# In the second up projection, one weight chunk in four gets its remainder from a DMA that adds instead of a subtraction on the vector engine

## The chip, the cores and the metric

The kernel runs on one core of one Trainium2 chip, in one launch. The core has five engines with instruction queues of their own: PE (matrix products, with weight loads PEld beside them), ACT (activations and copies), DVE (element-wise vector work), POOL and SP (here mostly issuers of DMAs). The queues are in order; engines wait for each other and for DMAs by semaphores. The metric is the time of one execution on the device in microseconds.

## What is computed

Two residual layers over 256 tokens of width 2048, in fp32: a gated mixer and a convolutional FFN, then attention with forget gates and a second FFN, and a final norm. The change touches the up projection of the second FFN, `xn @ w_up` below, with a weight of 2048 x 11264.

```python
def conv_ffn(xn, w_up, conv_w, conv_b, w_down):
    S = xn.shape[1]
    h = xn @ w_up
    hp = jnp.pad(h, ((0, 0), (CONV_W - 1, 0), (0, 0)))
    h = sum(hp[:, k:k + S] * conv_w[k] for k in range(CONV_W)) + conv_b
    gate, val = jnp.split(h, 2, axis=-1)
    return (jax.nn.silu(gate) * val) @ w_down
...
    for l in range(DEPTH):
        ...
        h = h + conv_ffn(rmsnorm(h, f_norm[l]), f_w_up[l], f_conv_w[l], f_conv_b[l], f_w_down[l])
```

## The kernel before

All weights are streamed from DRAM once, in chunks of 128 x 1024 fp32 (512 KB). A product in fp32 accuracy is made from products in the faster format fp32r: each operand is split into a rounded part and a remainder, and the products rounded x rounded, rounded x remainder and remainder x rounded are added up in PSUM. The activations X1 hold both parts side by side (2 x 256 columns). The weights are split as they stream by: for every chunk, ACT writes the rounded part `whi` (L95, a copy from `raw` into a tile of type fp32r), and DVE writes the remainder `wlo` = raw - whi (L96).

`Stream` keeps this in order. Each chunk is an item of a list; at step i it issues the load of item i + 6 on SP (L77), the split of item i + 3 (L95, L96), and the matmuls of item i, and then lets the waiting epilogues go one step further (`advance`). The buffers go round: `raw` has 4 (LOADS - AHEAD + 1), `whi` and `wlo` have 4 each (AHEAD + 1). So the load of a chunk into `raw` has to wait until the chunk four before it has been split, and a split has to wait until PE is through with the chunk four before it.

`feat_block` computes 256 features for all tokens from a block of K / 4 chunks of 128 x 1024: 4 chunks, c = 0 to 3, in the up projection. For a chunk PE runs first 16 products of 128 x 256 with `whi` (two halves of X1 for each of 8 weight tiles), then 8 with `wlo`. Sometimes some of the `whi` products are 512 wide. `ffn_up(l)` runs 44 such blocks for each layer; after blocks 1, 12, 23 and 34 an item without a load stands between (`between`, L676), and in layer 1 one after block 2 that starts `residual_by_token` (L384 to L398), which issues a 1024 KB load of gains on POOL and small DMAs on SP. Each block's epilogue `up_done` scales the sums (L350 to L357), convolves (L659, L663), applies SiLU and gate (L666, L667) and splits the result for the down projection (L283, L284), on ACT and DVE, while the next blocks run.

The order of the work on each engine is the order in which this code is written out; there is no scheduler behind it.

Of the kernel before, what the change touches and what calls it, by code (L numbers as in the profile page):

```python
# [10 lines left out]
F32 = mybir.dt.float32  # L11
F32R = mybir.dt.float32r
I32 = mybir.dt.int32
AF = mybir.ActivationFunctionType
OP = mybir.AluOpType
# [5 lines left out]
KD = D // P  # L21
# [22 lines left out]
class Stream:  # L44


    def __init__(self, nc, pool):
        self.nc, self.pool = nc, pool
        self.items, self.pending = [], []
        self.raw, self.parts = {}, {}  # L50

    def chunk(self, src, mult, at, at_load=None, at_split=None, rows=(1, 1), place=None):


        self.items.append((src, mult, at_load, at_split, at, rows, place))

    def then(self, at_load=None, at_split=None, at_mult=None):
        self.items.append((None, at_mult, at_load, at_split, 0, None, None))
# [21 lines left out]
    def _split(self, i):  # L80
        if self.items[i][3]:
            self.items[i][3]()
        raw = self.raw.pop(i, None)
        if raw is None:
            return
        at, (n, pitch) = self.items[i][4:6]
        hi, lo = (self.pool.tile([P, CHUNK + PAD], F32R, name=k, tag=k)[:, at:at + CHUNK] for k in ("whi", "wlo"))
        raw = raw.rearrange("p (n w) -> p n w", n=n)
        h, l = hi, lo
        if n > 1:  # L90
            h, l = (a[:, :n * pitch].rearrange("p (n w) -> p n w", n=n) for a in (h, l))
        else:
            h, l = h[:, None, :], l[:, None, :]
        h, l = (a[:, :, :raw.shape[2]] for a in (h, l))
        self.nc.scalar.activation(h, raw, AF.Copy)  # L95
        self.nc.vector.tensor_tensor(l, raw, h.bitcast(F32), op=OP.subtract)  # L96
        self.parts[i] = (hi, lo)

    def run(self):
# [46 lines left out]
def build(ctx, tc, d, out):  # L146
# [10 lines left out]
    h = const.tile([P, KD, T], F32, name="h")  # L157
    X1 = const.tile([P, KD, 2 * T], F32R, name="X1")
# [8 lines left out]
    s = Stream(nc, wpool)  # L167
    ph = Phase(tc)

    def main_ps():  # L170
        return psum.tile([P, 2, 512], F32, name="ps", tag="ps", bufs=3)
# [4 lines left out]
    def column(i):  # L176
        return col[:, i:i + 1]


    def mm(o, a, b, start, stop):  # L180
        nc.tensor.matmul(o, a, b, start=start, stop=stop, skip_group_check=True)  # L181
# [6 lines left out]
    def wide_next():  # L188
        return state["wide"].pop(0) if state["wide"] else 0

    def feat_block(src, x, K, done):

        box = {}
        n = K // 4
        for c in range(n):
            def mult(hi, lo, c=c):
                if c == 0:
                    box["ps"], box["both"] = main_ps(), False  # L200
                ps, xx, wide = box["ps"], x(), wide_next()
                box["both"] |= wide > 0

                def rounded(j, m):
                    nonlocal wide
                    w = hi[:, j * 256 + m * P:j * 256 + (m + 1) * P]
                    kt = 4 * c + j
                    if wide > 0:
                        mm(ps[:, m, :], w, xx[:, kt, :], kt == 0, False)
                        wide -= 1  # L210
                    else:
                        for half in range(2):
                            mm(ps[:, m, :T], w, xx[:, kt, half * T:(half + 1) * T], kt == 0 and half == 0, False)

                def remainder(j, m):
                    kt = 4 * c + j
                    mm(ps[:, m, :T], lo[:, j * 256 + m * P:j * 256 + (m + 1) * P], xx[:, kt, :T],
                       False, kt == K - 1)

                for product in (rounded, remainder):  # L220
                    for j in range(4):
                        for m in range(2):
                            product(j, m)
                if c == n - 1:
                    s.start(done(box["ps"], box["both"]))
            s.chunk(src[c], mult, FEAT_AT)

    def tok_block(src, x, done, K=KD):
        tok_blocks([(src, done)], x, K)
# [52 lines left out]
    def two_parts(dst, src):  # L282
        nc.scalar.activation(dst[..., :T], src, AF.Copy)  # L283
        nc.vector.tensor_tensor(dst[..., T:], src, dst[..., :T].bitcast(F32), op=OP.subtract)  # L284
# [65 lines left out]
    def scaled(ps, both, a):  # L350

        src = ps[:, :, :T]
        if both:
            nc.scalar.activation(a, ps[:, :, T:], AF.Copy)
            nc.vector.tensor_tensor(a, ps[:, :, :T], a, op=OP.add)
            src = a
        nc.vector.tensor_tensor(a, src, rB[:, None, :].to_broadcast([P, 2, T]), op=OP.mult)  # L357
# [26 lines left out]
    def residual_by_token():  # L384

        gains = ph.keep("gains", [P, D])
        nc.gpsimd.dma_start(gains, d["final"].to_broadcast([P, D]))
        ways = []
        for tb in range(2):
            for g in range(4):  # L390
                turned = blocks_turned(h[:, 4 * g:4 * g + 4, tb * P:(tb + 1) * P])
                yield
                ways.append(rows_out(f"h{tb}{g}", turned))
                yield
        for tb in range(2):
            for g in range(4):
                yield
                rows_in(by_token()[:, tb, g * 512:(g + 1) * 512].rearrange("p (r x) -> p r x", r=4), ways.pop(0))  # L398
# [243 lines left out]
    def ffn_h():  # L642
        ph.open(f"ffn{state['layer']}")
        return ph.keep("H", [P, KF, 2 * T], F32R)

    def up_done(l, i):
        def done(ps, both):
            state["layer"] = l
            H = ffn_h()
            while state["scaled"] <= l:  # L650
                yield
            a = ph.temp("a", [P, 2, T])
            scaled(ps, both, a)
            yield
            c = ph.temp("c", [P, 2, T])
            for m in range(2):
                f = m * KF + i
                w = [column(C_CONVW + (l * 3 + k) * 2 * KF + f) for k in range(3)]
                nc.scalar.activation(c[:, m, :], a[:, m, :], AF.Identity, scale=w[2],  # L659
                                     bias=column(C_CONVB + l * 2 * KF + f))  # L660
                for k in (1, 0):
                    n = 2 - k
                    nc.vector.scalar_tensor_tensor(c[:, m, n:], a[:, m, :T - n], w[k], c[:, m, n:],  # L663
                                                   op0=OP.mult, op1=OP.add)
            yield
            nc.scalar.activation(c[:, 0, :], c[:, 0, :], AF.Silu)  # L666
            nc.vector.tensor_tensor(c[:, 0, :], c[:, 0, :], c[:, 1, :], op=OP.mult)  # L667
            yield
            two_parts(H[:, i, :], c[:, 0, :])
        return done  # L670

    def ffn_up(l):
        for i in range(KF):
            feat_block(d[f"up{l}"][4 * i:4 * i + 4], lambda: X1, KD, up_done(l, i))
            if i % 11 == 1:
                s.then(at_mult=between)  # L676
            if l and i == 2:
                s.then(at_mult=lambda: s.start(residual_by_token()))
# [279 lines left out]
    for p in range(8):  # L958
        feat_block(d["a_in_u"][4 * p:4 * p + 4], lambda: X1, KD, u_done(p))
    for p in range(8):  # L960
        feat_block(d["a_out"][4 * p:4 * p + 4], mlp_x2, KD, residual(p, C_FNORM, row_scale))
    ffn_up(0)
    for p in range(8):
        feat_block(d["down0"][11 * p:11 * p + 11], ffn_h, KF, residual(p, C_BNORM))
# [13 lines left out]
    for p in range(8):  # L978
        feat_block(d["b_out"][4 * p:4 * p + 4], lambda: att("X2"), KD, residual(p, C_FNORM + KD, row_scale))
    ffn_up(1)  # L980
    s.then(at_mult=between)
    for blk in range(3):
# [72 lines left out]
```

## Time and profile before

| what | value |
|---|---|
| median of 3 runs | 2181.74 us (2180.86 to 2181.95) |
| profiled execution, its time as the profile gives it (span from the first to the last instruction) | 2179.9 us |
| difference of the median from that span | 1.8 us |
| mean granted clock of PE | 0.999 |
| DMA packets | 447.31 MB, mean 205 GB/s |
| loads `raw<-up` (both layers) | 352 of 512 KB, 4.1 us from issue to landing (median) |
| second up projection | from about 1453 us to 1932 us: 44 blocks of 4 chunks |

A row of the timeline gives the start, the duration, the engine, the line of the kernel, the operation and its tiles as out<-in; in brackets stands how long the engine was idle before, and who released it. A row of a group gives count, busy time, mean duration of one and the idle time before them. "To landing" is the time from a DMA's issue until its semaphore says that all of its data is there. The profile's busy times for PE are modelled at their ends, so a burst of matmuls can seem to reach a little into the next.

### The profile page before, as it was taken

What the parts mean: (1) busy time and instruction counts of PE and PEld (TensorE: products, weight loads), DVE (VectorE), ACT (ScalarE), POOL (GpSimd) and SP (SyncE); (2) the same over time, 40 slices, a digit from 0 to 9 for tenths busy, and PEclk for the clock granted to TensorE, in tenths of its full rate; (3) what the DMA queues carried; (4) which work ended last, traced back from release to release, by engine and by line L of the source; (5) the groups of instructions that cost most, each with busy time, mean ns of one, the idle gap of its engine ahead of it and who ended that gap; (6) DMA issues with size and microseconds to landing.
All of it is one profiled execution on the core that took longest, in us unless ns stands there. A gap on an engine that the chain in (4) does not pass through costs nothing.

```text
span 2179.9 us, 45085 instructions
## 1 busy us (share of the span) xinstructions
PE 2170.3 (100%) x18740; PEld 2154.6 (99%) x18740; DVE 1474.8 (68%) x2085; ACT 1145.4 (53%) x1536; POOL 26.9 (1%) x46
## 2 busy tenths in 40 slices
PE   9999999999999999999999999999999999999998
PEld 9999999999999999999999999999999999999998
DVE  6696687777777755556787676678777777764444
ACT  6665555555555544444545665446555555544443
POOL 0000000000000000000001100000000000000000
PEclk9999999999999999999999999999999999999999
DMA  8686566665666666666777776567766666666664
GB/s 311 191 241 202 193 198 195 189 199 190 198 193 194 195 190 199 193 195 184 244 244 257 232 224 200 185 216 228 240 195 194 193 195 189 201 191 194 193 192 153
DMA packets 153229, 447.31 MB, mean 205 GB/s; under 512 B 25584, under 2 KB 44800, under 8 KB 152640
## 3 DMA queue, kind: packets, MB, share of 16 engines
q1 hardware_dynamic: 151488, 440.48, 64.6%
q0 software_dynamic: 1072, 3.41, 0.6%
q8 instruction: 146, 2.39, 0.5%
q10 hardware_dynamic: 464, 0.55, 0.1%
q14 instruction: 59, 0.48, 0.1%
HBM read 430.72 MB, written 13.65 MB: 204 GB/s over the span
## 4 chain that ended last, share of the span: by engine, by line
PE 99%; DMA 0%; DVE 0%; ACT 0%; SPq 0%; issue 0%; DVEq 0%
PE ps L181 98%; PE mp L913 0%; PE ps L907 0%; PE ps L908 0%; PE ps L906 0%; PE mp L912 0%; DMA mlp_vt<-a_in_v 0%; DVE h L491 0%; PE mp L376 0%; ACT whi L95 0%; ACT sq L405 0%; PE mp L181 0%; DVE h L404 0%; SPq L496 0%; DVE h L486 0%
## 5 line engine op out<-in xcount | busy, mean ns | idle before, releaser
L96 DVE TENSOR_TENSOR wlo<-raw,whi 128x1024 fp32r<-128x1024 f32 (+1 forms) x778 | 945.1, 1219 | 462.4 <-ACT whi L95 458.2
L95 ACT ACTIVATE whi<-raw 128x1024 fp32r<-128x1024 f32 (+1 forms) x778 | 819.3, 1058 | 737.8 <-PE ps L181 660.3
L181 PE MATMUL ps<-X,whi 128*128 128x256 f32 (+1 forms) x6476 | 824.0, 279 | 0.0
L181 PEld LDWEIGHTS ps<-X,whi 128*128 128x128 f32 x6476 | 776.2, 188 | 6.5
L181 PE MATMUL ps<-X,wlo 128*128 128x256 f32 x3328 | 445.3, 276 | 0.0
L181 PEld LDWEIGHTS ps<-X,wlo 128*128 128x128 f32 x3328 | 409.9, 188 | 1.6
L181 PE MATMUL ps<-whi,ffn_H 128*128 128x256 f32 (+1 forms) x1402 | 222.7, 277 | 0.0
L181 PEld LDWEIGHTS ps<-whi,ffn_H 128*128 128x128 f32 x1402 | 192.0, 188 | 0.4
L181 PE MATMUL ps<-ffn_H,whi 128*128 128x256 f32 x1408 | 173.9, 276 | 0.0
L663 DVE SCALAR_TENSOR_TENSOR ffn_c<-ffn_a,col,ffn_c 128x255 f32<-128x255 f32 x352 | 161.9, 481 | 6.4
L181 PEld LDWEIGHTS ps<-ffn_H,whi 128*128 128x128 f32 x1408 | 166.1, 188 | 0.0
L181 PE MATMUL ps<-whi,att_X 128*128 128x256 f32 (+2 forms) x970 | 164.3, 285 | 0.0
L181 PE MATMUL ps<-whi,X 128*128 128x256 f32 (+1 forms) x1000 | 157.4, 280 | 0.4 <-ACT whi L95 0.4
L181 PE MATMUL ps<-wlo,ffn_H 128*128 128x256 f32 (+1 forms) x700 | 151.3, 277 | 0.0
L181 PEld LDWEIGHTS ps<-whi,att_X 128*128 128x128 f32 x970 | 135.4, 188 | 3.5
L181 PEld LDWEIGHTS ps<-whi,X 128*128 128x128 f32 x1000 | 133.5, 188 | 1.9 <-ACT whi L95 0.6
L357 DVE TENSOR_TENSOR ffn_a<-ps,rB 128x512 f32<-128x512 f32 x76 | 52.6, 692 | 116.1 <-PE ps L181 116.1
L659 ACT ACTIVATE ffn_c<-ffn_a,col 128x256 f32<-128x256 f32 x176 | 96.3, 594 | 50.0 <-DVE ffn_a L357 50.0
L181 PEld LDWEIGHTS ps<-wlo,ffn_H 128*128 128x128 f32 x700 | 112.0, 188 | 0.1
L181 PE MATMUL ps<-wlo,att_X 128*128 128x256 f32 (+2 forms) x476 | 105.4, 286 | 0.0
L181 PE MATMUL ps<-wlo,X 128*128 128x256 f32 (+1 forms) x498 | 98.1, 280 | 0.0
L181 PE MATMUL ps<-ffn_H,wlo 128*128 128x256 f32 x704 | 94.1, 276 | 0.0
(177 smaller groups left out, 1379.2 us busy)
## 6 DMA issues: line engine op xcount, KB each, us to landing
raw<-up SPq DMA_DIRECT2D x352, 512.0 KB, 4.1
raw<-down SPq DMA_DIRECT2D x154, 512.0 KB, 4.3
raw<-a_in_u SPq DMA_DIRECT2D x32, 512.0 KB, 4.6
raw<-a_out SPq DMA_DIRECT2D x32, 512.0 KB, 3.9
raw<-b_q SPq DMA_DIRECT2D x32, 512.0 KB, 4.7
raw<-kvf_v SPq DMA_DIRECT2D x32, 512.0 KB, 4.9
raw<-b_g SPq DMA_DIRECT2D x32, 512.0 KB, 4.4
raw<-b_out SPq DMA_DIRECT2D x32, 512.0 KB, 4.2
```

Of the source, the lines that this page charges most:

```text
L95: self.nc.scalar.activation(h, raw, AF.Copy)
L96: self.nc.vector.tensor_tensor(l, raw, h.bitcast(F32), op=OP.subtract)
L181: nc.tensor.matmul(o, a, b, start=start, stop=stop, skip_group_check=True)
L357: nc.vector.tensor_tensor(a, src, rB[:, None, :].to_broadcast([P, 2, T]), op=OP.mult)
L659: nc.scalar.activation(c[:, m, :], a[:, m, :], AF.Identity, scale=w[2], bias=column(C_CONVB + l * 2 * KF + f))
L663: nc.vector.scalar_tensor_tensor(c[:, m, n:], a[:, m, :T - n], w[k], c[:, m, n:], op0=OP.mult, op1=OP.add)
```

## The change

In the second layer's up projection, the second chunk of each block (c = 1) no longer has its remainder subtracted on DVE. ACT writes the negated rounded part into `wlo`, and a DMA issued on POOL then adds the fp32 chunk `raw` onto it, in place. All other chunks are split as before.

```diff
+        self.by_dma, self.added = False, {}
...
         self.items.append((src, mult, at_load, at_split, at, rows, place))
+        self.added[len(self.items) - 1] = self.by_dma
...
         self.nc.scalar.activation(h, raw, AF.Copy)
-        self.nc.vector.tensor_tensor(l, raw, h.bitcast(F32), op=OP.subtract)
+        if self.added[i]:
+            self.nc.scalar.activation(l, h.bitcast(F32), AF.Copy, scale=-1.0)
+            self.nc.gpsimd.dma_start(l[:, 0, :], raw[:, 0, :], accum_op=OP.add)
+        else:
+            self.nc.vector.tensor_tensor(l, raw, h.bitcast(F32), op=OP.subtract)
...
-    def feat_block(src, x, K, done):
+    def feat_block(src, x, K, done, by_dma=()):
...
+            s.by_dma = c in by_dma
             s.chunk(src[c], mult, FEAT_AT)
+            s.by_dma = False
...
-            feat_block(d[f"up{l}"][4 * i:4 * i + 4], lambda: X1, KD, up_done(l, i))
+            feat_block(d[f"up{l}"][4 * i:4 * i + 4], lambda: X1, KD, up_done(l, i), (1,) if l else ())
```

In the changed kernel the rounding is L97, the negated copy L99, the adding DMA L100, the subtraction L102 and the load L79; the lines of the epilogue are 8 higher than before.

On ACT, one block in the middle of the second up projection stands like this before the change (`whi<-raw` is the rounding of a chunk, `ffn_c` and `ffn_H` belong to the epilogue of an older block):

```order
L659 ACTIVATE ffn_c<-ffn_a,col 128x256 x2
L95 ACTIVATE whi<-raw 128x1024
L666 ACTIVATE ffn_c<-ffn_c 128x256
L95 ACTIVATE whi<-raw 128x1024
L283 ACTIVATE ffn_H<-ffn_c 128x256
L95 ACTIVATE whi<-raw 128x1024 x2
```

And in the changed kernel:

```order
L667 ACTIVATE ffn_c<-ffn_a,col 128x256 x2
L97 ACTIVATE whi<-raw 128x1024
L674 ACTIVATE ffn_c<-ffn_c 128x256
L97 ACTIVATE whi<-raw 128x1024
L99 ACTIVATE wlo<-whi 128x1024
L291 ACTIVATE ffn_H<-ffn_c 128x256
L97 ACTIVATE whi<-raw 128x1024 x2
```

The copy L99 has come in right behind the rounding of chunk c = 1, ahead of the older block's `ffn_H` and of the rounding of the next two chunks.

On SP, the loads of two blocks of the same stage, with what each waits for (DMAHW and a number: an earlier DMA of SP's; DVE: the subtraction that last read the raw buffer), before:

```order
L77 DMA raw<-up 128x1024 [waits DMAHW0_49,DVE_49]
L77 DMA raw<-up 128x1024 [waits DMAHW1_49,DVE_49]
L77 DMA raw<-up 128x1024 [waits DMAHW2_49,DVE_49]
L77 DMA raw<-up 128x1024 [waits DMAHW3_49,DVE_49]
L77 DMA raw<-up 128x1024 [waits DMAHW4_49,DVE_49]
L77 DMA raw<-up 128x1024 [waits DMAHW5_49,DVE_49]
L77 DMA raw<-up 128x1024 [waits DMAHW6_49,DVE_49]
```

And in the changed kernel (DMASW and a number: a DMA of POOL's):

```order
L79 DMA raw<-up 128x1024 [waits DMAHW0_49,DVE_49]
L79 DMA raw<-up 128x1024 [waits DMAHW2_49,DVE_49]
L79 DMA raw<-up 128x1024 [waits DMAHW1_49,DMASW5_49]
L79 DMA raw<-up 128x1024 [waits DMAHW3_49,DVE_49]
L79 DMA raw<-up 128x1024 [waits DMAHW4_49,DVE_49]
L79 DMA raw<-up 128x1024 [waits DMAHW6_49,DVE_49]
L79 DMA raw<-up 128x1024 [waits DMAHW5_49,DMASW6_49]
```

Every fourth load, that of a block's chunk c = 1, now waits for an adding DMA in place of DVE: it writes the buffer from which the adding DMA of the block before reads. The three loads after it are behind it in SP's queue.

On POOL, after the last work of the attention, before and then in the changed kernel:

```order
L892 AFFINE_SELECT att_big<-att_big 128x2x128 x2
L387 DMA ffn_gains<-final 128x2048
```

```order
L900 AFFINE_SELECT att_big<-att_big 128x2x128 x2
L100 DMA wlo<-raw 128x1024 x4
L395 DMA ffn_gains<-final 128x2048
L100 DMA wlo<-raw 128x1024 x40
```

The 44 adding DMAs stand on POOL around the load of the gains, which is now the fifth of them in line.

## The prediction

> **What bounds the kernel now.** I read the engine totals first, then the end of the chain in order of time, then the stretch in which the change acts.
>
> ```profile
> PE 2170.3 (100%) x18740; PEld 2154.6 (99%) x18740; DVE 1474.8 (68%) x2085; ACT 1145.4 (53%) x1536; POOL 26.9 (1%) x46
> 1461.79 710.41 PE ps L181 x6204
> 1500.00:1900.00 400.00, 400.00 (x3500) 398.68 (x3499) 292.63 (x414) 221.99 (x297) 0.00 (x0) 1.00 0.66 205
> ```
>
> The second row says that from 1461.79 us on, for 710 us, the chain that ends last is nothing but matmuls of L181: the whole second up projection lies in it. The third row is a stretch of 400 us inside that projection (busy time of PE, weight loads, DVE, ACT, POOL, then clock, DMA share, GB/s). PE is busy for 400.00 of 400 us at a granted clock of 1.00. So nothing that is taken off DVE (292.63 of 400) can shorten this stage: PE has no wait there to give back. What the change can do is leave PE as it is, or make it wait. To see which, I follow one changed chunk (the second of a block, c = 1) through the engines. Columns: start, duration, engine, line, tiles.
>
> ```profile
> 1697.60 1.07 PE L181 MATMUL ps<-X,wlo 128*128 128x256 f32 x8
> 1697.80 1.06 ACT L95 ACTIVATE whi<-raw 128x1024 fp32r<-128x1024 f32 x1 [1.28 <-PE ps L181]
> 1698.89 1.23 DVE L96 TENSOR_TENSOR wlo<-raw,whi 128x1024 fp32r<-128x1024 f32 x1 [0.51 <-ACT whi L95]
> ...
> 1700.15 0.33 SPq L77 DMA_DIRECT2D raw<-up  x1
> ...
> 1708.48 1.07 PE L181 MATMUL ps<-X,wlo 128*128 128x256 f32 x8
> 1708.69 1.06 ACT L95 ACTIVATE whi<-raw 128x1024 fp32r<-128x1024 f32 x1
> ```
>
> These rows hold two deadlines. At 1697.60 PE begins the remainder products of the c = 1 chunk of the block before; at 1697.80 ACT rounds the new c = 1 chunk, DVE subtracts until 1700.12, and PE needs that remainder only at 1708.48, one block (1708.48 - 1697.60 = 10.88 us) after the last such burst. **First deadline:** the remainder has 8.4 us to spare. **Second deadline:** 0.03 us after the subtraction ends, at 1700.15, SP issues the load of the next block's c = 1 chunk. There are four raw buffers and four chunks in a block, so this chunk always lands in the same buffer, and its load cannot start before the buffer's last reader is done. That load lands and its rounding starts at 1708.69.
>
> ```profile
> L77 SPq DMA_DIRECT2D raw<-up x147: 327/328/419, 1503.2 to 1898.8; - x147
> DMA to landing us min/median/max: 3.4/4.2/5.7
> ```
>
> With the median of 4.2 us it lands at 1704.4, so 4.3 us of this loop are slack today. The loop is: load, round, remainder, buffer free, next load; it must go round once per block of 10.88 us.
>
> **The change, part by part.** It takes 44 subtractions off DVE (44 x 1.22 us = 54 us), which are worth nothing, since PE never waits in this stage. It also puts 44 copies on ACT.
>
> ```profile
> L96 DVE TENSOR_TENSOR wlo<-raw,whi 128x1024 fp32r<-128x1024 f32 x147 | 179.2, 1221 | 46.5 <-ACT whi L95 46.2
> L95 ACT ACTIVATE whi<-raw 128x1024 fp32r<-128x1024 f32 x148 | 157.2, 1062 | 136.5 <-PE ps L181 135.1
> ```
>
> A copy of that shape takes 1.06 us; ACT is busy 221.99 of 400 us, so per block 6.0 of 10.88 us become 7.1. It is hidden in ACT's idle time (135.1 us of waiting for PE in these rows alone). Behind L99 on ACT stand the H part of an older block and the rounding of two more chunks, which have some 8 us before PE needs them: nothing. POOL had one DMA in this stage and gets 44 more; queued behind each on POOL is only the next one, and once the load of the gains (between the fourth and fifth add), which is read hundreds of us later. L99 itself waits for the remainder products of the block before (done at 1697.60 + about 0.9), which is before the rounding ends at 1698.86: nothing.
>
> What matters is that the remainder is now ready, and **the raw buffer free, only when the DMA has landed**. On SP the c = 1 load waits for that DMA instead of DVE, and the loads of the next three chunks are queued behind it. The new loop is
>
> load + 1.06 (L97) + 1.06 (L99) + x (the adding DMA, issue to landing) + 4 handovers.
>
> A handover is 0.03 us in the rows above (1700.12 to 1700.15); I take 0.05 each, an estimate, 0.2 in all. Four loads then leave in a bunch on queues that have run dry, so I take a load between the smallest 3.4 and the median 4.2: 3.8 us. No adding DMA stands in this trace, so x is bounded by POOL's other DMAs:
>
> ```profile
> L855 POOL DMA_DIRECT2D att_cB<-cd x16: 537/554/557, 1155.3 to 1259.9; - x16
> DMA to landing us min/median/max: 3.2/4.8/6.4
> ...
> att_cB<-cd POOLq DMA_DIRECT2D x16, 128.0 KB, 4.8
> ffn_gains<-final POOLq DMA_DIRECT2D x1, 1024.0 KB, 6.4
> ```
>
> Low end 3.2 us (the fastest of 16 that move a quarter of the bytes). High end 10.6 us: the 6.4 of 1024 KB, and behind it, if the sum is written only after both sources are read, a transfer like a load (4.2). I take **6.4**, the row of 1024 KB: an add must read 512 KB of raw and 512 KB of the negated part, so 1024 KB go in.
>
> By the Trainium skill (Collectives: The Full Stack, "The bandwidth ceiling: the fold count and why AG ≠ RS ≠ AR"), an add in the DMA engines costs not the arithmetic but a second source read; no run shown here has an add to test that.
>
> Sum: loop = 3.8 + 1.06 + 1.06 + 6.4 + 0.2 = 12.52 us against 10.88, so 1.64 us late per block once the slack is used up. First and last changed chunk:
>
> ```profile
> 1447.13 1.06 ACT L95 ACTIVATE whi<-raw 128x1024 fp32r<-128x1024 f32 x1 [0.53 <-ACT whi L95]
> ...
> 1926.21 1.07 PE L181 MATMUL ps<-X,wlo 128*128 128x256 f32 x8
> ```
>
> The first is rounded by 1448.19 and negated by 1449.3; 43 loops later, 1449.3 + 43 x 12.52 = 1987.7, the last add is issued, and it lands at 1994.1, where PE wants it at 1926.21: **68 us late**. The profiled execution would go from a span of 2179.9 to 2247.8; the median of the runs, 2181.74, lies 1.8 us above that span, so I forecast 2181.74 + 68 = **2250 us**. What moves it: 43 us of time for each us of x or of load.
>
> **Rivals.**
>
> *Hidden (not slower).* The loop fits if load + x is at most 10.88 - 2.12 - 0.2 = 8.56, with a load of 3.8 an x of 4.76; the slack at the start allows 4.85. Then PE never waits, since the first deadline alone (8.56 us from the end of L99, 1699.92, to 1708.48) is far looser. For it: the fastest of the 16 took 3.2 us, and in the new loop the add runs while few loads are in flight. Against: the median for a quarter of the bytes is 4.8. Time: 2181.7. The Trainium skill (DMA: Bandwidth & Descriptors, "Anatomy of one DMA — SWDGE (gpsimd) path") fits a POOL-issued DMA as 2.0 us and the bytes at 436 GB/s; an estimate by it is 3.2 us for 512 KB and 4.4 for 1024 KB, which gives this rival. The trace disagrees: its 1024 KB took 6.4, its 128 KB 4.8 where the fit gives 2.3. Chance 0.27.
>
> *A slow add.* x = 10.6: loop 16.72, end 1449.3 + 43 x 16.72 + 10.6 - 1926.2 = 253 us late, 2434 us. From x = 8.56 on, PE also misses the first deadline in the first block already. For it: the add is a read, a sum and a write of the same bytes. Against: no row as long for a transfer of this size. Chance 0.13.
>
> *The streams collide.* In the page's slices, GB/s:
>
> ```profile
> GB/s 311 191 241 202 193 198 195 189 199 190 198 193 194 195 190 199 193 195 184 244 244 257 232 224 200 185 216 228 240 195 194 193 195 189 201 191 194 193 192 153
> ```
>
> The stage moves 205 GB/s at a DMA share of 0.66. An add per block puts 1024 KB of reads on top, 1.05 MB in 10.88 us = 96 GB/s, 301 in all, near the most that any slice of the profile shows (311, in the first). If loads then take the stage's longest 5.7, with x = 6.4 the loop is 14.4 and the end 149 us late: 2331 us. Against: in the new loop the add comes when its bunch of loads has largely landed. Chance 0.11.
>
> *It doesn't do what it says*, for instance ACT becomes the bound: 7.1 of 10.88 us per block says no, and all 44 DMAs stand in POOL's order. 0.01, time unchanged.
>
> **How the numbers follow.** Forecast (x between 5.0 and 8: by the same sum 6 to 138 us late, 2188 to 2320) 0.47, hidden 0.27, slow 0.13, collision 0.11, not as said 0.01, faster 0.01 (there is no PE wait to remove). The likeliest of these is the forecast: 2250. The range runs from the hidden case, 2179, to 2350, which takes in the collision and, with the load of 3.8, an x of up to 8.7; it leaves out the slow add and little else. A change within 0.2% (4.4 us) cannot be told from none by a measurement of this kernel: 0.28 (hidden and not as said); slower 0.71; faster 0.01. The likeliest case's own range is 2188 to 2320.
>
> **What would show it.** Right: the landing time of L100 is near 6 us and the sum of load, 2.12 and landing exceeds 10.88; SP's longest waits are for the DMA into wlo; PE in the same stage has a wait once a block, of that excess, before the remainder (or the first) products of c = 1; DVE's waits grow, nothing else changes outside 1450 to 1930 us. Wrong: PE is still busy through the whole stage (then x is below 4.8 us), or PE waits while the loop sum stays below 10.88 (then something else is late: the rounding of other chunks on ACT, or loads of the chunks behind on SP), or the lost time lies outside this stage.

## The result, and the profile after

The changed kernel takes **2198.72 us** (median of 4 runs, 2196.41 to 2200.07), the kernel before 2181.47 us beside it (2180.86 to 2181.95): ratio 1.0078, 95% interval 1.0066 to 1.009, 17 us slower. The direction was forecast and the time lies in the range; the size (68 us) was not.

The page of the changed kernel (span 2197.0 us, profiled execution 2198.89 us), three rows: the engine totals, the shares of the chain that ended last, and the group of the remainder products:

```profile
PE 2178.1 (99%) x18740; PEld 2161.2 (98%) x18740; DVE 1427.3 (65%) x2041; ACT 1191.2 (54%) x1580; POOL 63.8 (3%) x90
PE 95%; DMA 3%; ACT 1%; issue 0%; DVE 0%; POOL 0%; DVEq 0%; ACTq 0%; POOLq 0%; SPq 0%
L187 PE MATMUL ps<-X,wlo 128*128 128x256 f32 x3328 | 447.5, 277 | 9.4 <-DMA wlo<-raw 8.8
```

PE's chain is no longer unbroken: PE stands idle for 8.8 us before remainder products, waiting for the adding DMA. The stretch that the prediction looked at, by the windows view (us; busy time of PE, PEld, DVE, ACT, POOL; clock, DMA share, GB/s), now has two faces:

```profile
1500.00:1600.00 100.00, 91.21 (x757) 90.18 (x756) 58.24 (x87) 55.92 (x73) 6.72 (x8) 0.98 0.87 257
1600.00:1930.00 330.00, 330.00 (x2878) 328.66 (x2877) 205.30 (x306) 215.61 (x277) 25.38 (x30) 1.00 0.84 242
```

From 1600 us on PE is as busy as before (330.00 of 330), with an adding DMA in every block. The loss lies ahead of that. Two rows of the start of the c = 1 remainder products, in blocks 13 and 43 of the changed kernel, and the same burst of block 13 before (block 43's, at 1926.21, stands in the prediction), all from the timeline:

```profile
1616.51 1.07 PE L187 MATMUL ps<-X,wlo 128*128 128x256 f32 x8
...
1943.04 1.07 PE L187 MATMUL ps<-X,wlo 128*128 128x256 f32 x8
```
```profile
1599.68 1.07 PE L181 MATMUL ps<-X,wlo 128*128 128x256 f32 x8
```

1616.51 - 1599.68 and 1943.04 - 1926.21 are both 16.83 us: blocks 13 to 43 lose nothing. Followed from block to block, the lateness is 0.8 us in blocks 0 to 2 (it was there before the first add), 1.6 in block 3, 4.1 in 5, 7.4 in 7, 10.4 in 8, 13.2 in 9, 15.6 in 10 and 16.8 from 13 on. So **16.0 us are lost in blocks 3 to 12**, between about 1490 and 1610 us. What stands there and nowhere else in the stage is the token exchange started after block 2 (`residual_by_token`: 32 DMAs of 64 KB and 8 of 256 KB on SP). The adding DMAs of the two stretches, 1500 to 1600 and 1600 to 1930 us, issue to landing:

```profile
L100 POOL DMA_DIRECT2D wlo<-raw x8: 838/840/846, 1509.0 to 1596.8; - x8
DMA to landing us min/median/max: 4.8/7.2/9.5
```
```profile
L100 POOL DMA_DIRECT2D wlo<-raw x30: 843/846/862, 1607.9 to 1923.9; - x30
DMA to landing us min/median/max: 4.7/5.0/7.0
```

By these medians an undisturbed add takes 5.0 us, not the 6.4 that the prediction took; in the stretch with the exchange, whose DMAs are issued from 1494.7 to 1569.5 us, it takes 7.2.

Why doesn't the forecast loop run in every block? The sections on the kernel and on the change said that the raw buffers go round and that the load of chunk c = 1 is the one that waits for the add. As built, that the buffers go round is true of the kernel before, in all 44 blocks. In the changed kernel the next block's c = 1 load mostly takes the buffer of c = 2, which a subtraction frees and no DMA, and the load that waits for the adding DMA (DMASW in the rows on SP shown there) is mostly that of **c = 2**. The trace agrees: for 35 of the 43 adds that a further block follows, the load that waits for the add is the third of the next block's four, and the rounding of c = 1 waits for the second. How many chunks after the add's own chunk its buffer is taken again, block by block in the built program:

```
block   0 1 2 3 4 5 6 7 8 9 10 11 12 13 14..23 24 25..34 35 36..43
before  4 4 4 4 4 4 4 4 4 4  4  4  4  4    4    4    4    4    4
after   5 5 4 4 5 5 4 4 4 5  5  5  5  4    5    4    5    4    5
```

Where it is five, the late load is of a chunk without an add, and the loop doesn't feed itself. Only after blocks 6, 7 and 8 does the next c = 1 chunk load three times running into the buffer of the add before (after blocks 2 and 3 twice), and there the loop runs as forecast. The adds of blocks 6 to 9, and one turn of the loop (loads, rounding, negated copy, add):

```profile
1520.47 0.84 POOL L100 DMA_DIRECT2D wlo<-raw  x1 [10.65 <-ACT ffn_H L291]
1533.69 0.84 POOL L100 DMA_DIRECT2D wlo<-raw  x1 [12.38 <-ACT wlo L99]
...
1545.52 1.06 ACT L97 ACTIVATE whi<-raw 128x1024 fp32r<-128x1024 f32 x1 [4.93 <-DMA raw<-up]
1546.61 1.06 ACT L99 ACTIVATE wlo<-whi 128x1024 fp32r<-128x1024 f32 x1
1547.97 0.84 POOL L100 DMA_DIRECT2D wlo<-raw  x1 [13.44 <-ACT wlo L99]
...
1562.55 0.84 POOL L100 DMA_DIRECT2D wlo<-raw  x1 [13.75 <-ACT wlo L99]
```

The steps from add to add are 13.2, 14.3 and 14.6 us, against 10.88 for a block. From the add at 1533.69 to the rounding at 1545.52 pass 11.8 us (landing and load), then 1.06 and 1.06 on ACT and 0.3 until POOL issues.

Part of the loss is no wait at all. From the starts of successive matmuls between 1475 and 1960 us: seven gaps of over 0.6 us cost 10.6 us; 747 matmuls of 256 columns that follow at 117.8 ns rather than 113.3 cost 3.4; 14 at about 213 ns cost 1.4; 0.7 lie between. The first wait shows the second term (the `whi` bursts have 16 matmuls each):

```profile
1489.81 1.98 PE L187 MATMUL ps<-X,whi 128*128 128x256 f32 x16
1492.40 1.18 PE L187 MATMUL ps<-X,wlo 128*128 128x256 f32 x8 [0.61 <-DMA wlo<-raw]
1493.42 2.05 PE L187 MATMUL ps<-X,whi 128*128 128x256 f32 x16
1495.30 1.11 PE L187 MATMUL ps<-X,wlo 128*128 128x256 f32 x8
```

A burst takes 2.05 us after the wait, 1.98 ahead of it.

### The profile page after: what moved, and what is told of

It reads as the page before. It is cut to its first block, busy times and chain, and to the rows that moved or that the text cites. A ratio compares the mean times of both kernels' runs of the same rounds, so it can differ in the third digit from the quotient of the medians.

```text
span 2197.0 us, 45207 instructions
## 1 busy us (share of the span) xinstructions
PE 2178.1 (99%) x18740; PEld 2161.2 (98%) x18740; DVE 1427.3 (65%) x2041; ACT 1191.2 (54%) x1580; POOL 63.8 (3%) x90
## 4 chain that ended last, share of the span: by engine, by line
PE 95%; DMA 3%; ACT 1%; issue 0%; DVE 0%; POOL 0%; DVEq 0%; ACTq 0%; POOLq 0%; SPq 0%
PE ps L187 94%; DMA wlo<-raw 2%; DMA raw<-up 1%; ACT whi L97 0%; ACT wlo L99 0%; PE mp L921 0%; PE mp L532 0%; PE ps L916 0%; PE ps L915 0%; PE ps L914 0%; PE mp L920 0%; DVE wlo L102 0%; DVE ffn_turned L700 0%; ACT ffn_H L291 0%; DVE ffn_c L671 0%
## 5 line engine op out<-in xcount | busy, mean ns | idle before, releaser
L97 ACT ACTIVATE whi<-raw 128x1024 fp32r<-128x1024 f32 (+1 forms) x778 | 819.3, 1058 | 718.0 <-PE ps L187 601.1
L102 DVE TENSOR_TENSOR wlo<-raw,whi 128x1024 fp32r<-128x1024 f32 x734 | 892.8, 1221 | 451.6 <-ACT whi L97 444.2
L187 PEld LDWEIGHTS ps<-X,wlo 128*128 128x128 f32 x3328 | 411.4, 188 | 12.2 <-issue 9.0
```

## The experiments

Each kernel was timed beside the kernel before (2181.3 to 2181.5 us in every group); "lost in the stage" is the lateness of block 43 less that of block 2, measured as above in the profiled execution.

| kernel | median us (range) | ratio, 95% interval | lost in the stage, us |
|---|---|---|---|
| changed kernel | 2198.72 (2196.41 to 2200.07) | 1.0078 [1.0066, 1.009] | 16.0 |
| e1_late | 2181.39 (2180.58 to 2181.88) | 0.9999 [0.9989, 1.0008] | none |
| e2_early | 2195.18 (2193.75 to 2195.6) | 1.0061 [1.0046, 1.0076] | 14.0 |
| e3_strict | 2216.19 (2209.3 to 2219.26) | 1.0148 [1.013, 1.0165] | 37.2 |
| e4_crossed | 2240.42 (2237.86 to 2244.21) | 1.0271 [1.0255, 1.0286] | not used |
| e4b_crossed | 2189.91 (2188.68 to 2191.11) | 1.004 [1.0028, 1.0053] | 7.7 |
| e5_noexch | 2186.76 (2182.06 to 2187.52) | 1.0022 [1.0013, 1.0031] | 1.6 |
| e6_copy | 2190.31 (2189.83 to 2192.73) | 1.0044 [1.0032, 1.0057] | 9.7 |
| e7_wide | 2196.39 (2196.06 to 2197.38) | 1.007 [1.0058, 1.0083] | 15.3 |
| e4c_queue | 2191.94 (2189.44 to 2193.05) | 1.0042 [1.003, 1.0055] | 8.2 |
| e9_noexch_wide | 2184.16 (2183.23 to 2188.5) | 1.0014 [1.0005, 1.0023] | 2.1 |
| e10_both | 2191.48 (2189.25 to 2194.89) | 1.0043 [1.003, 1.0056] | 7.7 |
| e11_queue | 2190.3 (2189.12 to 2192.95) | 1.004 [1.0026, 1.0053] | 6.6 |
| e13_tiny | 2184.93 (2183.26 to 2188.21) | 1.0019 [1.001, 1.0028] | 2.4 |
| e14_later | 2195.61 (2191.04 to 2197.91) | 1.0063 [1.005, 1.0075] | 16.1 |

### Where the loss lies: half of the change each

The edit of e1_late; e2_early has `i < 13` in its place:

```diff
-            feat_block(..., up_done(l, i), (1,) if l else ())
+            feat_block(..., up_done(l, i), (1,) if l and i >= 13 else ())
```

> The add by DMA in blocks 13 to 43 only. Theory (the loss needs the token exchange that runs beside blocks 4 to 10): within 3 us of the kernel before, 2181 to 2184 us, PE without a wait for an adding DMA. Rival (the forecast's loop of 12.5 us in every block): 30 blocks x 1.64 us = +45 us or so, 2220 to 2230 us. The adding DMA should land in 4.7 to 5.3 us here.

> The add by DMA in blocks 0 to 12 only. Theory (exchange): nearly the whole loss stays, 2195 to 2200 us, with 10 us of PE waits and the slower matmuls behind them. Rival (loop in every block): 12 x 1.64 = +18 us, less than the slack at the start, 2195 to 2200 too; only together with the run of the late blocks does it tell the two apart.

The 31 late adds cost nothing (2181.39 against 2181.32 us); the 13 early ones 14 of the 17 us (132 matmuls there come at 117.8 ns, not 747). Windows of e1_late:

```profile
1490.00:1610.00 120.00, 120.00 (x1050) 119.56 (x1050) 90.19 (x132) 69.28 (x93) 1.76 (x2) 1.00 0.78 240
1610.00:1930.00 320.00, 320.00 (x2805) 319.12 (x2804) 199.39 (x298) 208.46 (x267) 24.84 (x29) 1.00 0.84 243
```

PE is busy in all of 320 us beside 29 adds, so the prediction's loop costs nothing in this stretch, and neither the extra copies on ACT nor the DMAs' bytes cost anything by themselves. The subtractions that DVE no longer does are worth nothing, as forecast.

### The forecast loop, made to run

`slots` are four fixed tiles, `taken` counts the loads:

```diff
-            place = self.pool.tile([P, CHUNK], F32, name="raw", tag="raw", bufs=LOADS - AHEAD + 1)
+            place = self.slots[self.taken % len(self.slots)]
+            self.taken += 1
```

> The changed kernel with four fixed raw buffers taken strictly in turn, so that the next block's c = 1 load always waits for this block's adding DMA, as the prediction assumed. Theory of the loop (load + round + negate + add + handovers goes round once per block): some 0.4 us per block late in the quiet blocks (5.0 + 3.7 + 2.12 + 0.45 = 11.3 against 10.88) and 2 to 3 us per block beside the exchange: +30 to +45 us, 2210 to 2227 us. Rival (only the DMA engines' load beside the exchange matters, which buffer is taken does not): unchanged, 2196 to 2200 us.

Measured 2216.19 us. With the four buffers strictly in turn, as the prediction had them, 21.0 us are lost up to block 10 and 16.2 more after it. What PE waits for, and four adds far from the exchange:

```profile
PE ps L191 <- DMA wlo<-raw: 20.2, 19, 3.1
```
```profile
1711.09 0.84 POOL L104 DMA_DIRECT2D wlo<-raw  x1 [11.73 <-ACT ffn_H L295]
1721.57 0.85 POOL L104 DMA_DIRECT2D wlo<-raw  x1 [9.64 <-ACT wlo L103]
1732.67 0.84 POOL L104 DMA_DIRECT2D wlo<-raw  x1 [10.25 <-ACT wlo L103]
1744.89 0.85 POOL L104 DMA_DIRECT2D wlo<-raw  x1 [11.38 <-ACT wlo L103]
```

The loop takes 10.5, 11.1 and 12.2 us here, and 11.4 on average from block 13 on: just over a block's 10.88. Its parts there, as medians of 30 turns in the trace, are 5.0 us for the add, 0.05 until the load is issued, 3.5 for the load and 2.5 from its landing to the next add; the prediction had 6.4, 0.05, 3.8 and 2.27. So its loop exists where the buffers do go round, and of its terms the add was the one far off. The whole is worth 35 us by the medians, not 68, and in the profiled execution more than half is lost beside the exchange.

### The buffers' order beside the exchange

A first kernel, e4_crossed, was meant to keep the add's buffer from the next chunk c = 1 throughout. In every second block its c = 1 load stood ahead of the split of the chunk whose buffer it took, so those chunks were overwritten before they were read, and the loads waited in another order; its time says nothing on the question.

> The changed kernel with four fixed raw buffers in which c = 1 and c = 2 change places from block to block, so that the c = 1 load never waits for the last adding DMA and the c = 2 load always does. Theory of the loop: the waits at blocks 7 to 10 go, what is left is at most 5 us, 2182 to 2187 us. Rival (contention alone): the adds beside the exchange are as late as before, 2196 to 2200 us.

In e4b_crossed the split stands ahead of that load:

```diff
+            place = self.slots[(self.taken + self.crossed.get(i, 0)) % len(self.slots)]
...
+            if late:
+                self._split(i + AHEAD)
             if 0 <= i + LOADS < n:
                 self._load(i + LOADS)
...
+            s.cross, s.late = ({1: 1, 2: -1}.get(c, 0) if swap == 2 else 0), swap > 0 and c == 1
```

> Four fixed raw buffers, and the buffers of chunks 1 and 2 change places in every second block of the last up projection, so that the buffer an adding DMA reads is always taken next by chunk 2 of the block after, five chunks later, never four. Theory (the loss comes where the next chunk 1 has to load into the buffer of the add before it, three blocks in a row beside the token exchange): that loop is cut everywhere, so no wait of 2 us or more of the matmuls for a remainder is left, and the time is 2182 to 2187 us. Rival (the exchange's traffic makes the adding DMAs and loads late by itself, whichever buffer they use): the waits at blocks 7 to 10 stay and the time is 2195 to 2200 us.

Measured 2189.91 us, between the two: 8.3 of the 16.0 us are gone, and no wait is longer than 1.2 us (PE's wait, then the landing of the adds between 1500 and 1600 us):

```profile
PE ps L197 <- DMA wlo<-raw: 4.2, 6, 1.2
```
```profile
DMA to landing us min/median/max: 5.1/7.1/9.0
```

Both expectations missed, and both theories held in part: **half of the loss is the add's buffer being taken next by the chunk that adds again; the other half stays with adds that land at 7 us**. In e4b_crossed the split also stands ahead of the c = 1 load, from block 1 on. A second kernel keeps the changed kernel's splits and gets the same order of buffers from block 4 to 12 in another way, from issuing the exchange's 40 DMAs on ACT's queue:

```diff
-                ways.append(rows_out(f"h{tb}{g}", turned))
+                ways.append(rows_out(f"h{tb}{g}", turned, nc.scalar))
```

> As the changed kernel, but the token exchange's 40 DMAs are issued from ScalarE's queue. In the order as built, the buffer of the adds of blocks 4 to 12 is then taken next by chunk 2 of the block after throughout (five chunks on), where in the changed kernel blocks 6, 7 and 8 have four. If the buffers in turn and SyncE's queue are what costs: 2182 to 2187 us. If the traffic costs by itself what the crossed buffers left: 2188 to 2192 us. If the place of the exchange's issues and the buffers' order don't matter: 2196 to 2200 us.

2190.3 us: as much is gone. What remains isn't quite the same there: 4.6 of its 6.6 us lie in blocks 3 to 5. The adds between 1500 and 1600 us land in 5.1 us (median), but the five issued between 1512 and 1557 us, beside the exchange, take 5.1 to 6.7.

### What in the exchange makes the other half

e5_noexch leaves out the exchange's transposes and DMAs, e13_tiny keeps all its instructions and moves a sixteenth of its bytes, e4c_queue issues it from ACT, e14_later starts it after block 19. All but the first build on e4b_crossed. The cores of the edits of e5_noexch, e13_tiny and e14_later, in this order:

```diff
-                turned = blocks_turned(h[:, 4 * g:4 * g + 4, tb * P:(tb + 1) * P])
-                ways.append(rows_out(f"h{tb}{g}", turned))
...
-                ways.append(rows_out(f"h{tb}{g}", turned))
+                ways.append(rows_out(f"h{tb}{g}", turned, 8))
...
-            if l and i == 2:
+            if l and i == 19:
```

> The token exchange in the last up projection is left out (its transposes and its 40 DMAs; the output is then not the reference's), the adding DMAs stay in all 44 blocks. Theory (the loss needs the exchange's traffic beside it): 2181 to 2184 us, adding DMAs landing in 4.7 to 5.6 us throughout, no wait of the matmuls over 1 us for a remainder. Rival (the loss belongs to the first dozen blocks, to the buffers' order or the lead they begin with, with or without the exchange): 2190 to 2199 us.

> As the kernel with the crossed buffers (2189.9 us), with every DMA of the token exchange in its place but moving 8 of each 128 columns, a sixteenth of the bytes (the output is then not the reference's); transposes, waits and the number of issues stay. If the exchange's bytes on the DMA engines make the 8 us that are left: 2182 to 2185 us, adds landing in 4.8 to 5.6 us between 1500 and 1600 us. If its issues in SyncE's queue, or the transposes, make them: 2188 to 2192 us.

> As the kernel with the crossed buffers (2189.9 us), and the token exchange's 40 DMAs are issued from ScalarE's queue in place of SyncE's; their bytes are the same. What is left there (8 us) comes either from SyncE's queue, in which the loads of the chunks stand behind the exchange's DMAs and behind the loads that wait for an add, or from the traffic itself, which makes loads and adds land late. If it is the queue: 2182 to 2185 us. If it is the traffic: 2188 to 2192 us, with adding DMAs of 7 us and more between 1500 and 1575 us as there.

> As the kernel with the crossed buffers (2189.9 us), with the token exchange begun after block 19 rather than block 2. If the exchange costs wherever it stands: 2188 to 2192 us, the waits beginning beyond block 19. If the early place matters (in block 3 the rounding of chunk 1 comes 14.0 us after that of block 2, in the middle of the stage 10.9, so the add begins late): 2182 to 2186 us, with no wait of the matmuls for a remainder in blocks 3 and 4, and little from block 20 on.

Without the exchange 1.6 us are lost in the profiled execution (2183.99 us), nearly all in blocks 3 and 4, and adds land in 4.9 us. The median of 2186.76 missed both expectations; more on it below. This kernel takes away both causes at once: in its trace the adds of blocks 6 to 8, too, hold up the load of c = 2 of the next block, so the distance there is five and not four. The bytes alone are told apart by e13_tiny, where the order of the buffers is that of e4b_crossed: with the exchange's instructions in place and few of its bytes the loss is 2.4 us, median 2184.93, as expected of the bytes. The adds and loads of e4b_crossed and then of e13_tiny between 1500 and 1600 us (KB each, median us to landing):

```profile
raw<-up SPq DMA_DIRECT2D x36, 512.0 KB, 5.6
wlo<-raw POOLq DMA_DIRECT2D x9, 512.0 KB, 7.1
```
```profile
raw<-up SPq DMA_DIRECT2D x37, 512.0 KB, 4.7
wlo<-raw POOLq DMA_DIRECT2D x9, 512.0 KB, 5.3
```

So it is the exchange's **bytes on the DMA engines** that make adds and loads late, not its transposes nor its issues. Nor is it the 1024 KB load of the gains on POOL, which stays in both kernels. Moving the issues from SP to ACT gained nothing (2191.94 against 2189.91 us); that run alone couldn't have told why, since the adds then land at 6.0 us (median), earlier than before, while the issues now take ACT's time (in e11_queue 1.8 to 3.7 us for four).

e14_later missed upwards. The first wait, in block 3, stays without any exchange beside it, and the waits of the exchange move with it to blocks 24 to 26; the rest is told under the slower matmuls. That first wait needs no contention. In the kernel before, block 3 rounds its c = 1 chunk late, and its remainder products follow soon; the third row is the add of block 3 in the changed kernel:

```profile
1483.22 1.04 ACT L95 ACTIVATE whi<-raw 128x1024 fp32r<-128x1024 f32 x1
```
```profile
1490.81 1.07 PE L181 MATMUL ps<-X,wlo 128*128 128x256 f32 x8
```
```profile
1486.72 0.87 POOL L100 DMA_DIRECT2D wlo<-raw  x1 [13.38 <-ACT wlo L99]
```

The first two are 7.6 us apart. Rounding and copy (2 x 1.06), 0.5 us until POOL issues and an add of 5.7 us (1486.72 to the burst at 1492.40 shown above) come to 8.3: 0.7 us late, near the 0.7 to 1.1 us by which block 3 falls back in the kernels with early adds other than e6_copy.

### The price of an add

```diff
-            self.nc.gpsimd.dma_start(l[:, 0, :], raw[:, 0, :], accum_op=OP.add)
+            self.nc.gpsimd.dma_start(l[:, 0, :], raw[:, 0, :])
```

> The DMA of the one chunk in four copies the fp32 chunk over the negated rounded part in place of adding it (the remainder is then not formed; everything else as in the changed kernel). Theory (an add in the DMA costs hardly more than a copy from the same queue, what counts is that the chunk waits for a second transfer): landing 4.5 to 5.0 us in the quiet part after 1600 us, time 2194 to 2199 us. Rival (reading the destination and adding is what makes it long): landing 3.2 to 4.0 us, time 2182 to 2190 us.

The landing came out as the rival had it, the time 0.3 us above the rival's range. From 1600 us on:

```profile
L100 POOL DMA_DIRECT2D wlo<-raw x31: 528/528/537, 1600.3 to 1927.2; - x31
DMA to landing us min/median/max: 2.9/3.6/5.5
```

A copy of 512 KB lands in 3.6 us, the add in 5.0. The queue rows of the pages say why: POOL's queue in e6_copy, in the changed kernel, and in the kernel before (packets, MB, share of the 16 DMA engines over the span).

```profile
q0 software_dynamic: 7408, 26.48, 3.5%
```
```profile
q0 software_dynamic: 7408, 26.48, 6.3%
```
```profile
q0 software_dynamic: 1072, 3.41, 0.6%
```

For the same bytes and packets the adds hold the engines for 5.7% of the span, the copies for 2.9%: an add takes twice a copy's time on the DMA engines. The Trainium skill's rule that the prediction named (Collectives: The Full Stack, "The bandwidth ceiling: the fold count and why AG ≠ RS ≠ AR"), that an add costs a second source read, agrees with that ratio. Its fit (DMA: Bandwidth & Descriptors, "Anatomy of one DMA — SWDGE (gpsimd) path"), 3.2 us for 512 KB as an estimate, is near the copy's 3.6 and not the add's 5.0. The shorter transfer takes 8.4 us off the time. The 9 us that stay are lost from block 4 to block 13 again: beside the exchange even a plain second transfer behind each of these loads is too long.

### The slower matmuls

```diff
                 if c == n - 1:
                     s.start(done(box["ps"], box["both"]))
+                    if again:
+                        between()
```

e7_wide adds this to the changed kernel, e9_noexch_wide to e5_noexch, e10_both to e4b_crossed, at the end of blocks 3 or 4 to 12; each call makes the first ten `whi` matmuls of the next block 512 columns wide, in place of twenty of 256.

> As the changed kernel, with the first 10 rounded products of each of blocks 5 to 13 of the last up projection as 512-column matmuls (the same columns in half the instructions). Theory (after a wait the matmuls run 4% slow, 117.8 in place of 113.3 ns each, because the weight loads have lost their lead, until 512-column matmuls give it back): a burst of 16 matmuls that begins after these is back at 1.98 to 1.99 us in blocks 5 to 13 rather than 2.05, the time falls by 2 to 4 us to 2194 to 2197 us. Rival (the slower matmuls have another cause, such as the traffic beside them): the rows stay at 2.05 us, the time at 2197 to 2200 us.

> As the kernel without the token exchange (runs between 2182.1 and 2187.5 us, its profiled run 2184.0), with 512-column matmuls at the head of blocks 5 to 13. Theory (its slower runs are those in which a wait of under 1 us in block 3 or 4 left the matmuls at 117.8 ns, which at the next 512-column matmuls, about 110 us on, has cost 110 x 4% = 4.4 us): no run above 2185 us, median 2181 to 2184 us. Rival (the slower runs have another cause): the runs lie as before, median 2186 to 2188 us.

> As the kernel with the crossed buffers (2189.9 us; in its profile some 390 matmuls at 117.8 ns, 1.8 us), with 512-column matmuls at the head of blocks 4 to 13. Theory (the two remedies act on different terms and add): 2187 to 2189 us. Rival (matmuls at 113.3 ns only arrive earlier at the next wait): 2189.5 to 2191 us.

In e7_wide the slower rate ends at the 512-column matmuls: 285 matmuls at 117.8 ns are left of 747, 1.3 us of loss rather than 3.4 (those at 213 ns cost 2.8 rather than 1.4). The time fell by 2.3 us to 2196.39, in the range of the theory, though the intervals of the two kernels overlap and the stage lost only 0.7 us less in the profiled execution. e10_both gained nothing (2191.48 against 2189.91 us), 0.5 us above the rival's range. e9_noexch_wide is half a confirmation: 9 of 11 runs lie between 2183.2 and 2185.2 us, where e5_noexch had 6 of 11 above 2186.7; two lie higher (2187.37 and 2188.5), and of the second, which is the profiled one, 4.4 us were there before the stage began.

The clearest view of the slower rate came unasked, in e14_later. PE there around its first wait, and 107 us later at the next 512-column burst, the `between` after block 12:

```profile
1491.38 1.18 PE L197 MATMUL ps<-X,wlo 128*128 128x256 f32 x8 [0.81 <-DMA wlo<-raw]
1492.39 2.05 PE L197 MATMUL ps<-X,whi 128*128 128x256 f32 x16
...
1596.98 2.05 PE L197 MATMUL ps<-X,whi 128*128 128x256 f32 x16
1598.86 1.11 PE L197 MATMUL ps<-X,wlo 128*128 128x256 f32 x8
1599.81 2.02 PE L197 MATMUL ps<-X,whi 128*128 128x512 f32 x8
...
1605.35 1.98 PE L197 MATMUL ps<-X,whi 128*128 128x256 f32 x16
1607.17 1.07 PE L197 MATMUL ps<-X,wlo 128*128 128x256 f32 x8
```

One wait of 0.8 us, and every burst after it takes 2.05 us until 512-column matmuls come; block 13 has fallen back 4.2 us from block 3 with no wait named between them. The same happened again beside the exchange: from 1691.5 us, where one matmul followed after 180 ns and no wait is named, to the `between` after block 23, and from 1755.7 us, behind a wait of 1.97 us, to that after block 34. Not only 512-column matmuls end it: at 1738.5 us it ended at a single interval of 329 ns. All together are 2086 matmuls at 117.8 ns, 9.3 of the 16.1 us lost. Two windows show that the granted clock has no part in it (clock and DMA share are the third and second figures from the end):

```profile
1494.00:1606.00 112.00, 112.00 (x944) 111.56 (x943) 66.78 (x100) 69.46 (x90) 8.54 (x10) 1.00 0.83 236
1616.00:1676.00 60.00, 60.00 (x532) 60.00 (x531) 35.51 (x54) 38.99 (x50) 5.73 (x7) 1.00 0.86 248
```

The DMA share is about the same in both, so nothing here points to the traffic either. This also fits e5_noexch, whose upper runs are about 4 us above its lower ones, as one short wait followed by the slower rate would make them; its profiled execution was one of the lower, so that is argued and not shown. Some of them may instead have lost their time ahead of the stage, as e9_noexch_wide's profiled execution did; one of the 15 runs of the kernel before that stood beside it, too, took 2185.87 us.

## Why the prediction was right in direction and wrong in size

- **The direction:** right, but in part by luck. It owes most to a transfer that the prediction didn't look at: with the exchange left out (e5_noexch) the changed kernel is 5.4 us slower than the kernel before, little more than the 4.4 us that the prediction called indistinguishable from none.
- **PE bounds the stage, and 44 subtractions less on DVE are worth nothing:** right. e1_late is the cleanest proof, 0.9999 with 31 of them gone.
- **ACT's copies and POOL's queue cost nothing by themselves:** right; e1_late again.
- **The first deadline is loose (8.4 us to spare):** right from block 13 on, where the landing of 5.0 us leaves slack. In block 3 it failed (7.6 us where 8.3 are needed), and beside the exchange with adds of up to 9.5 us.
- **"There are four raw buffers and four chunks in a block, so this chunk always lands in the same buffer":** this step failed. It holds of the kernel before and was carried over unproved. In the changed kernel the next c = 1 chunk takes the buffer of c = 2, after 35 of the 43 blocks that another follows. The load that waits for the add is then of a chunk that adds nothing. e3_strict shows what the step was worth: with the buffers in turn the time is 2216 us, loss in every part of the stage; with them as built, nothing is lost in blocks 13 to 43. The rows to see it by stood in the built order on SP, in the section on the change. Besides the buffer's last reader, a load waits for the earlier load into the same buffer: before, the DMAHW numbers run 0, 1, 2, 3, in the changed kernel 0, 2, 1, 3. The second and the third load have changed buffers, and it is the third, c = 2, that waits for the add.
- **The adding DMA takes 6.4 us:** too long by 1.4 where nothing else runs. The bounds (3.2 and 10.6) held; the 1024 KB row was the wrong neighbour. By the prediction's own sum, x = 5.0 gives a loop of 11.12 us; e3_strict's turns from block 13 on average 11.4. So even with the buffers in turn this term was mis-sized, by 1.4 us in each loop of a forecast excess of 1.64.
- **The rival "the streams collide"** was closest to what happened, with another partner: not the stage's own loads, but the exchange's 4 MB, which were never looked at, put adds at 7.2 us and made the loop 13.2 to 14.6 us in the three blocks where it ran.
- **The signs named in advance:** SP's waits for the DMA into `wlo` are there, one per block and up to 8.9 us:

```profile
SPq L79 <- DMA wlo<-raw: 143.8, 44, 8.9
```

  PE's wait once a block is not (6 waits in 44 blocks). The sum of load, 2.12 and landing exceeds 10.88 nearly everywhere: from 1600 us on the medians give 4.6 + 2.12 + 5.0 = 11.7 us, and PE waits for nothing, since there the three don't form a loop. So the sign "PE is still busy" came true from block 13 on, though not for the reason given, an x below 4.8 us.

In the account of the 16.0 us: 8 to 9 come from blocks 6 to 8, where the buffer went to the next adding chunk (e4b_crossed and e11_queue, two ways to the same order, lose 7.7 and 6.6); of the rest, all but some 2 go with the exchange's bytes (e13_tiny); the last 2 are the first waits in blocks 3 and 4 (e5_noexch). Some 5 us of the whole (3.4 + 1.4) are not waiting but slower matmuls behind the waits; what ending them would give back is less sure, 2.3 us in e7_wide and nothing in e10_both. The four in a row at blocks 6 to 8 comes with the exchange's DMAs on SP's queue: it is gone when they are left out (e5_noexch) and when ACT issues them (e11_queue). How the built order comes to it stays open, since the distance was read off the built programs and not derived. No version beats the kernel before: PE is at 100% of the stage there, and the best of the changed ones (e1_late) equals it.

## What to carry over

When a change makes a buffer's last reader slower, find in the built program which transfer takes that buffer next; "four buffers, four chunks" isn't enough, since here the next chunk mostly took another buffer. Price a new DMA in the worst stretch of its stage, beside whatever else moves bytes there, not in the middle of it. And count more than the wait itself: on a PE-bound stage one wait of 0.8 us was followed by 4 us of slower matmuls.

## What was not expected of the hardware

- After a wait of PE, matmuls of 256 columns can follow at 117.8 rather than 113.3 ns at a granted clock of 1.00, for up to 110 us; it ended at 512-column matmuls (e14_later, e7_wide), and once at an interval of 329 ns. Not every wait starts it: in e7_wide one of 0.75 us in block 3 did not, in the changed kernel one of 0.61 us did. The cause stays open. A lost lead of the weight loads, the theory behind e7_wide, doesn't show in the trace of e14_later: at both rates the load for the next matmul starts 2 to 5 ns after a matmul's start.
- For some 3 us after some of the longer waits the clock is lower, and matmuls come 213 ns apart; the changed kernel after its wait at 1555.64 us:

```profile
1556.00:1560.00 4.00, 4.00 (x25) 4.00 (x25) 0.00 (x0) 0.00 (x0) 0.00 (x0) 0.65 0.87 263
```

- An adding DMA between two SBUF tiles of 512 KB lands in 5.0 us undisturbed, a copy in 3.6, and the add takes twice the copy's time on the DMA engines.
